# Token statistics taken from x^T, and attention operands transposed ahead on VectorE, in a hybrid convolution, attention and retention block

## The chip, the cores and the metric

The kernel runs on one core of a Trainium2 chip. Its time is that of one execution on the device, in microseconds (us); the smaller, the better. The engines are TensorE (PE, matrix products, with PEld for its weight loads), VectorE (DVE), ScalarE (ACT), GpSimd (POOL), and SyncE (SP), which here only issues DMAs. Each engine works off its own list of instructions in order.

## The reference

One layer of a trunk with 1024 tokens and 16 meta tokens put ahead of them, width 1024. All three groups of mixers read the same normalized input through one projection, and their outputs go through one output projection:

```
h = concat([meta, x])                         # 1040 x 1024
u = rms_norm(h, ln_w)                         # h * rsqrt(mean(h*h) + eps) * ln_w
cx, cb, cc, cz, cq, ckv, krope, mz, rq, rk, rv, rz = split(u @ w_in)
y_conv = cb * (conv_b + sum_j w[j] * (cc*cx)[t-2+j]) * silu(cz)
q = rms_norm(rms_norm(cq) @ w_uq)             # 8 heads of 96 (64 + 32 with rope)
k = rms_norm([rms_norm(ckv) @ w_ukv, krope])
o_mla = softmax(q k^T / sqrt(96), chunk causal) v * silu(mz)
o_ret = retention(rq, rk, rv) * silu(rz)      # 4 heads of 64, chunks of 64
h + concat([y_conv, o_mla, o_ret]) @ w_out    # without the meta tokens
```

All data are float32.

## The kernel before

Every large product is made in three: both factors are split into a high part, rounded to the PE's fp32r format, and a low part, the remainder (`split`: the high part on ACT, L103 or L106, the low part on DVE or POOL, L104, and L107 where a scale is applied), and `mm3` (L112) adds high x high, high x low and low x high. Products of 512 columns are the bulk of PE's work.

The stages follow one another in this order on PE:

- *Gate products* (`mz`, 0 to 55 us). x^T comes in eight tiles `xs` of 128 x 1040 (one per block k of 128 input features), which are split into `xah`, `xal`, `xbh`, `xbl`; the gate weights `ws_mz` come per k and are split into `wh_mz`, `wl_mz` (the low part on POOL for k = 2 and 5, else on DVE). The accumulators are eight tiles of 128 x 512, (b, g) for b = 0 to 3 and g = 0, 1; five of them are summed while the tiles arrive, the other three afterwards by `rest`.
- *Token statistics*. The mean square of a token is needed for each token as a row (`rb`, for tiles with tokens on the columns) and as a column (`r`). The kernel loads x once more with tokens on the partitions (`xt`, 16 loads of 256 KB on SP, L227), squares it on ACT with a running sum, and forms `vx`, `r` and, by a product with ones, the row `rps` (L243).
- *Latent projection* (`A`, 55 to about 135 us): weights `ws_A`, products `A`, and per block of tokens `a_lat` and `a_up`, which norm, apply rope and store q, k and v of all heads to DRAM (`q_s`, `k_s`, `v_s`), tokens on the rows.
- *Retention* (two units of 9 blocks, to about 245 us), *convolution* (two units, `conv_cx`, `conv_cz`, `conv_cb`, to about 343 us).
- *Attention* (to 531 us). The heads run one after the other; scores run four blocks ahead of the rest of a head. A head's operands `kT`, `qT` (features on the partitions, high and low, two buffers of each for alternate heads) are made by `qk_t` (L662): q and k of a pair of heads are loaded (`load_pair`), four 128 x 96 blocks are transposed on PE into PSUM (L668), and split from there on ACT and DVE. Heads 0 and 1 are prepared among the last convolution products, head h + 2 in four steps within head h.
- *Output projection* (to the end).

The gate results are finished one after the other behind the statistics (`mzz`, L257 to L260) and stored to DRAM (`mz_s`) on SP. The code gives the engines' work in program order, and a scheduler of the framework orders each engine's list ahead of time from this and from the dependencies; a `tc.issue_after` keeps an instruction behind another in that order.

Of the kernel before, what the change touches and what calls it, by code (L numbers as in the profile page):

```python
# [35 lines left out]
V_LN, V_QA, V_KVA, V_QN, V_KN, V_CW, V_CB, V_RN = 0, 8, 10, 11, 12, 13, 19, 21  # L36
NV = 22
# [13 lines left out]
def trunk(tc, ins, outs):  # L51
# [15 lines left out]
    NA, NW, GA = 4, 8, 0  # L67
# [13 lines left out]

    vec = cp.tile([P, NV], F32, name="vec")
# [12 lines left out]
    wqk = cp.tile([P, 1], F32, name="wqk")  # L95
# [13 lines left out]
    def mm3(out, l_, r_, first, last):  # L109

        for i, (x_, y_) in enumerate(((l_[0], r_[0]), (l_[0], r_[1]), (l_[1], r_[0]))):
            nc.tensor.matmul(out, lhsT=x_, rhs=y_, start=first and i == 0, stop=last and i == 2)  # L112
# [57 lines left out]
    with tc.tile_pool(name="ps0", bufs=1, space=PSUM, reuse_waits="tile") as ps0:  # L170
# [3 lines left out]
        warm2 = ps0.tile([P, 512], F32, tag="rps", name="warm2", bufs=2)  # L174
# [4 lines left out]
        def rest(b, g, a):  # L179
            for k in range(KT):  # L180
# [37 lines left out]
        ssh = cp.tile([P, 2, 9], F32, name="ssh")  # L218
        nc.gpsimd.memset(ssh, float(D // 2))
        for g, ts_ in enumerate(((0, 1, 2, 3), (4, 5, 6, 7), (8,))):  # L220
            for t in ts_:
                rows = NM if t == 8 else P
                src = meta_d if t == 8 else x_d[t * P:t * P + P]
                for j in range(2):
                    xt = work(("t3", "t4")[j], f"xt{t}_{j}")
# [3 lines left out]
            if g == GA:  # L229
                with tc.issue_after(last_t.ins):  # L230
                    wA = [load_w("A", k) for k in range(NA)]
            gs = slice(ts_[0], ts_[-1] + 1)
            nc.vector.tensor_tensor(vx[:, gs], ssh[:, 0, gs], ssh[:, 1, gs], op=ALU.add)
            nc.vector.tensor_scalar(vx[:, gs], vx[:, gs], 1.0 / D, EPS, op0=ALU.mult, op1=ALU.add)
            rsqrt(r[:, gs], vx[:, gs], len(ts_))
            if g == 2:
                break

            dg = work("t2", f"dg{g}").rearrange("p (t q) -> p t q", t=4)
            rps = ps0.tile([P, 512], F32, tag="rps", name=f"rps{g}", bufs=2)  # L240
# [8 lines left out]
        rest(2, 1, accs[2, 1])  # L249
        for g in range(2):  # L250
            accs[3, g] = ps0.tile([P, 512], F32, tag="rps", name=f"mz3{g}", bufs=2)
            rest(3, g, accs[3, g])
        for b in range(4):
            for g in range(2):
                z = work(("t3", "t4")[g], f"mzz{b}{g}")
# [4 lines left out]
                nc.sync.dma_start(mz_s[b][:, g * 512:g * 512 + 512], z)  # L260
# [8 lines left out]
    with tc.issue_after(last_t.ins):  # L269
        wA += [load_w("A", k) for k in range(len(wA), KT)]  # L270
# [4 lines left out]
    for i, (src, u_, j, sc) in enumerate([(wuq_d[:, 0, :], uq, 0, V_QA), (wuq_d[:, 1, :], uq, 1, V_QA + 1),  # L275
# [3 lines left out]
        with tc.issue_after(last_t.ins):  # L279
# [7 lines left out]
    nc.gpsimd.tensor_tensor(wqk, vec[:, V_QN:V_QN + 1], vec[:, V_KN:V_KN + 1], op=ALU.mult)  # L287
# [12 lines left out]

    def a_lat(t, ps):
# [5 lines left out]
        nc.vector.tensor_copy(c[R, c0:416], ps[R, c0:416])  # L307
# [95 lines left out]
    for t in [8] + list(range(NT)):  # L403
# [4 lines left out]
        if t == 3:  # L408
            wr = [[load_w("r0", k) for k in range(KT)]]
# [11 lines left out]
    oz = {}  # L421
# [9 lines left out]
    def r_rope(u, t, ps):  # L431
# [6 lines left out]
        nc.scalar.activation(rtf[R, cs], ps[R, cs], AF.Copy, scale=r[R, t:t + 1])  # L438
# [8 lines left out]
        nc.vector.tensor_tensor(qk[R, hs], qk[R, hs], tmp[R, hs], op=ALU.add)  # L447
# [87 lines left out]
    def feat(u, b, lo_, n, name):  # L535
# [3 lines left out]
        step()  # L539
        return pp  # L540

    def load_pair(hp):
        qt = hp_pool.tile([P, NT, 192], F32, tag="q", name=f"q{hp}")
        kt = hp_pool.tile([P, NT, 192], F32, tag="k", name=f"k{hp}")
        vt = hp_pool.tile([P, NT, 128], F32, tag="v", name=f"v{hp}")
        nc.sync.dma_start(kt, k_s.rearrange("t p c -> p t c")[:, :, hp * 192:hp * 192 + 192])
        nc.sync.dma_start(qt, q_s.rearrange("t p c -> p t c")[:, :, hp * 192:hp * 192 + 192])
        nc.sync.dma_start(vt, v_s[:SEQ, hp * 128:hp * 128 + 128].rearrange("(b p) c -> p b c", p=P))
        return qt, kt, vt
# [3 lines left out]
    def conv_cx(u, g, b):  # L553
# [3 lines left out]
        for lo_, n in (((NM - 2, 258), (NM + 256, 256)) if g == 0 else ((HA, 512),)):  # L557
# [11 lines left out]
    def conv_cz(u, g):  # L569
# [424 lines left out]
```

## Time and profile before

| | us |
|---|---|
| time, median of 3 runs | 579.41 |
| lowest and highest | 579.18, 580.03 |
| the profiled execution, its own time | 581.55 |
| its span in the profile | 579.8 |
| PE busy | 569.8 |
| DVE, ACT, POOL busy | 330.9, 255.0, 224.1 |

The rows come from one profiled execution, whose span begins with its first instruction; its own time is 1.75 us longer than the span. A row names a line of the kernel, the engine, the operation, and the tiles written and read, without the numbers of buffers.

### The profile page before, as it was taken

What the parts mean: (1) busy time and instruction counts of PE and PEld (TensorE: products, weight loads), DVE (VectorE), ACT (ScalarE), POOL (GpSimd) and SP (SyncE); (2) the same over time, 40 slices, a digit from 0 to 9 for tenths busy, and PEclk for the clock granted to TensorE, in tenths of its full rate; (3) what the DMA queues carried; (4) which work ended last, traced back from release to release, by engine and by line L of the source; (5) the groups of instructions that cost most, each with busy time, mean ns of one, the idle gap of its engine ahead of it and who ended that gap; (6) DMA issues with size and microseconds to landing.
All of it is one profiled execution on the core that took longest, in us unless ns stands there. A gap on an engine that the chain in (4) does not pass through costs nothing.

```text
span 579.8 us, 9595 instructions
## 1 busy us (share of the span) xinstructions
PE 569.8 (98%) x3401; PEld 481.7 (83%) x3401; DVE 330.9 (57%) x761; ACT 255.0 (44%) x616; POOL 224.1 (39%) x330
## 2 busy tenths in 40 slices
PE   8999999999999999999999999999999999999997
PEld 5877899988888888898898888898888888876886
DVE  5547768888536432553332667675757857664132
ACT  6765535665234332532010438475655646543000
POOL 2023258677103220151242968443524334624000
PEclk9999999999999999999999999999999999999999
DMA  8887513274703200130030648235112223113096
GB/s 326 289 265 241 182 67 120 108 224 158 234 1 92 74 0 19 54 110 18 20 97 1 199 145 273 73 103 171 56 38 73 77 71 128 37 68 116 1 301 224
DMA packets 46657, 70.39 MB, mean 121 GB/s; under 512 B 3792, under 2 KB 21840, under 8 KB 46480
## 3 DMA queue, kind: packets, MB, share of 16 engines
q1 hardware_dynamic: 43008, 63.47, 33.8%
q10 hardware_dynamic: 3600, 6.29, 2.9%
q8 instruction: 27, 0.44, 0.3%
q14 instruction: 22, 0.18, 0.1%
HBM read 48.75 MB, written 21.00 MB: 120 GB/s over the span
## 4 chain that ended last, share of the span: by engine, by line
PE 83%; DMA 9%; DVE 3%; ACT 2%; issue 2%; POOL 0%; SPq 0%; DVEq 0%; ACTq 0%; POOLq 0%
PE r L112 16%; PE S L112 9%; PE cv L112 8%; PE part L112 7%; PE A L112 6%; PE o L765 6%; PE pTp L724 5%; PE cz L112 4%; PE cb L112 4%; DMA out<-ot 4%; PE out L112 3%; PE qps L112 3%; DMA xs<-in_xT 2%; DMA xt<-in_x 2%; PE rsp L477 1%
## 5 line engine op out<-in xcount | busy, mean ns | idle before, releaser
L702 ACT ACTIVATE pr<-S,smx 128x144 f32<-128x144 f32 (+8 forms) x72 | 50.4, 701 | 27.3 <-DVE smx L693 13.4
L693 DVE TENSOR_REDUCE smx<-S 128x1 f32<-128x144 f32 (+8 forms) x72 | 49.8, 701 | 15.7 <-PE S L112 6.3
L710 POOL TENSOR_SCALAR pm<-pr,smx 128x16 f32<-128x16 f32 x64 | 18.4, 288 | 85.2 <-DVE smx L708 61.3
L711 POOL TENSOR_SCALAR pr<-pr,smx 128x128 f32<-128x128 f32 (+3 forms) x64 | 48.1, 752 | 0.6 <-DVE smx L708 0.6
L724 PE MATMUL pTp<-ident,pr 128*128 128x128 f32 x288 | 45.4, 274 | 1.5 <-ACT pt L730 1.4
L730 ACT COPY pt<-pTp 128x512 f32<-128x512 f32 (+2 forms) x64 | 31.8, 505 | 26.3 <-PE pTp L724 24.9
L451 POOL TENSOR_SCALAR kw<-qk,con 128x64 f32<-128x64 f32 (+1 forms) x36 | 13.8, 397 | 71.7 <-DVE qk L447 58.4
L724 PEld LDWEIGHTS pTp<-ident,pr 128*128 128x128 f32 x288 | 35.0, 140 | 7.0 <-POOL wol L104 1.8
L765 PEld LDWEIGHTS o<-pt,v 128*64 128x64 f32 x448 | 26.5, 137 | 12.1 <-issue 4.7
L765 PE MATMUL o<-pt,v 128*64 128x256 f32 (+2 forms) x448 | 36.2, 309 | 0.0
L112 PE MATMUL r<-wh_r,xal 128*128 128x512 f32 (+1 forms) x80 | 30.5, 381 | 0.0
L112 PE MATMUL r<-wh_r,xah 128*128 128x512 f32 (+1 forms) x80 | 30.4, 380 | 0.0
L112 PE MATMUL part<-woh,yh 128*128 128x512 f32 x64 | 30.1, 470 | 0.0
L112 PE MATMUL r<-wl_r,xah 128*128 128x512 f32 (+1 forms) x80 | 30.0, 375 | 0.0
L882 DVE SCALAR_TENSOR_TENSOR ot<-out,xr 128x512 f32<-128x512 f32 (+1 forms) x17 | 11.2, 660 | 31.1 <-DMA out<-ot 16.8
L112 PE MATMUL r<-wl_r,xbh 128*128 128x512 f32 x64 | 26.1, 409 | 0.0
L112 PE MATMUL r<-wh_r,xbh 128*128 128x512 f32 x64 | 25.7, 401 | 0.0
L112 PE MATMUL part<-wol,yh 128*128 128x512 f32 x64 | 25.5, 399 | 0.0
L112 PE MATMUL r<-wh_r,xbl 128*128 128x512 f32 x64 | 25.5, 398 | 0.0
L112 PE MATMUL part<-woh,yl 128*128 128x512 f32 x64 | 25.2, 394 | 0.0
L773 DVE TENSOR_TENSOR ym<-o,ym 64x256 f32<-64x256 f32 x32 | 13.5, 421 | 16.7 <-PE o L767 16.2
L104 POOL TENSOR_TENSOR wol<-wos,woh 128x512 fp32r<-128x512 f32 x16 | 20.4, 1291 | 2.6 <-ACT woh L103 2.6
(295 smaller groups left out, 1716.1 us busy)
## 6 DMA issues: line engine op xcount, KB each, us to landing
xt<-in_x SPq DMA_DIRECT2D x16, 256.0 KB, 4.5
ws_r<-in_win SPq DMA_DIRECT2D x16, 256.0 KB, 3.3
ws_c<-in_win SPq DMA_DIRECT2D x16, 256.0 KB, 2.9
wos<-in_wout SPq DMA_DIRECT2D x16, 256.0 KB, 3.8
xp<-in_x SPq DMA_DIRECT2D x16, 256.0 KB, 2.7
p_s<-xp SPq DMA_DIRECT2D x16, 256.0 KB, 2.0
xr<-p_s SPq DMA_DIRECT2D x15, 256.0 KB, 4.5
out<-ot ACTq DMA_DIRECT2D x15, 256.0 KB, 4.5
```

The lines of the kernel that those rows point to most:

```text
L104: (lo_eng or nc.vector).tensor_tensor(lo, src, hi.bitcast(F32), op=ALU.subtract)
L112: nc.tensor.matmul(out, lhsT=x_, rhs=y_, start=first and i == 0, stop=last and i == 2)
L451: nc.gpsimd.tensor_scalar(kw[R, j], qk[R, 2 + j], con[R, kd0 + j:kd0 + j + 1], 1.0, op0=ALU.mult, op1=ALU.mult)
L693: nc.vector.tensor_reduce(sm[:, i // 2:i // 2 + 1], sp[:, :n, :w], axis=AX.XY, op=ALU.max, negate=True)
L702: e = nc.scalar.activation(pr[:, c0:c1].rearrange("p (b c) -> p b c", b=n), sp, AF.Exp, bias=mx, accum_out=sm[:, 5 + i:6 + i])
L710: nc.gpsimd.tensor_scalar(pm[(2 * h + t // 4) % 2][:, t % 4, :NM], pr[:, nk - NM:nk], sm[:, 9:10], 1.0, op0=ALU.mult, op1=ALU.mult)
L711: nc.gpsimd.tensor_scalar(pr[:, :nk - NM], pr[:, :nk - NM], sm[:, 9:10], 1.0, op0=ALU.mult, op1=ALU.mult)
L724: tr_ = nc.tensor.transpose(out=tp[:, b * P:b * P + P], in_=pr[:, c0:c0 + P], identity=ident)
L730: nc.scalar.copy(pt[:, b0:b0 + nb, tt], src)
L765: nc.tensor.matmul(op[64 * cg:64 * cg + 64, c0:c1], lhsT=lv, rhs=src[:, i_, c_], start=b == 0, stop=False)
L773: nc.vector.tensor_tensor(ys, op[64 * cg:64 * cg + 64, :256].rearrange("p (a c q) -> p a c q", a=2, q=64), ys, op=ALU.mult)
L882: nc.vector.scalar_tensor_tensor(ot, acc[:, c0:c1], 0.5, xt, op0=ALU.mult, op1=ALU.add)
```

## The change

- *Statistics.* The loads `xt` and their squares go. ACT squares each x^T tile (`xsq`; the first one straight into the tile that later holds the constants, `con`), POOL adds the seven others to it, and nine products of 128 (or 16) tokens by a column of ones (`ssp`) sum over the features. The constants are loaded into `con` afterwards.
- *Weights and gate stores.* The loads of the A weights follow the last x^T tile; the gate results are kept and stored last. The remaining gate products run over k outside. Warm-up products: 11 instead of 8.
- *Queries and keys.* `qk_t` goes. `turn` handles k or q of a pair of heads in four parts, in slots spread over retention, convolution and the first steps of attention (`BEGIN`): it loads 128 x 8 x 192 from `k_s` or `q_s`, transposes it in blocks of 32 x 32 on DVE, splits it, and stores high and low part to DRAM (`T_s`). `load_head` fetches a head's `kT` and `qT` from there in 12 DMAs of 32 x 4 x 256 (128 KB).
- *Smaller ones.* The copy of `A` out of PSUM moves from DVE to ACT, one product in the convolution stands earlier on POOL, and the scale of some output weights is applied within the split.

The core of the diff:

```diff
-        accs = {bg: ps0.tile([P, 512], F32, name=f"mz{bg[0]}{bg[1]}") for bg in ((2, 1), (2, 0), (1, 1), (1, 0), (0, 1), (0, 0))}
+        ssp = bank("m31", "ssp")
...
+            if k == 0:
+                nc.scalar.activation(con[:, :L], st, AF.Square)
+            else:
+                sq = hp_pool.tile([P, L], F32, tag="v", name=f"xsq{k}")
+                nc.scalar.activation(sq, st, AF.Square)
+                nc.gpsimd.tensor_tensor(con[:, :L], con[:, :L], sq, op=ALU.add)
...
-                    with tc.issue_after(last_x.ins):
-                        last_t = nc.sync.dma_start(xt[:rows], src[:, j * 512:j * 512 + 512])
-                    nc.scalar.activation(xt[:rows], xt[:rows], AF.Square, accum_out=ssh[:rows, j, t:t + 1])
...
+        for t in range(9):
+            t0, rows = tok(t)
+            nc.tensor.matmul(ssp[:rows, t:t + 1], lhsT=con[:, t0:t0 + rows], rhs=ones[:, :1], start=True, stop=True)
...
-                nc.sync.dma_start(mz_s[b][:, g * 512:g * 512 + 512], z)
+                store.append((mz_s[b][:, g * 512:g * 512 + 512], z))
+        for x in store:
+            nc.sync.dma_start(*x)
...
-        nc.vector.tensor_copy(c[R, c0:416], ps[R, c0:416])
+        act[0] = nc.scalar.copy(c[R, c0:416], ps[R, c0:416]).ins
...
+    def turn(i, part):
+        hp, which = i // 2, 1 - i % 2
+        if part == 0:
+            src = hp_pool.tile([P, NT, 192], F32, tag="q", name=f"ts{i}")
...
+            for j, y in enumerate(x.rearrange("(j n r) c -> j r n c", j=4, r=32)):
+                nc.sync.dma_start(src[32 * j:32 * j + 32], y)
...
+                nc.vector.transpose(dst[:, 3 * j:3 * j + 3].rearrange("p c (n k) -> p n c k", k=32),
+                                    turned[i][0][:, :, 96 * j:96 * j + 96].rearrange("p n (c k) -> p n c k", k=32))
...
+    def load_head(h):
+        for which in (1, 0):
+            for x, src in zip((qT, kT)[which][h % 2], T_s[which][h // 2]):
...
+                for c in range(3):
+                    nc.sync.dma_start(x[32 * c:32 * c + 32, o:o + SEQ].bitcast(F32).rearrange("p (i r) -> p i r", i=4), src[3 * (h % 2) + c])
...
-            for j in range(4):
-                nc.tensor.transpose(out=tp[:96, j * P:j * P + P], in_=src[:, 4 * g + j, cs], identity=ident)
```

Three places in the engines' lists. The first is POOL at the start, from the product of two norm vectors (`wqk`) on: before, two low parts of gate weights stand there, and then the powers of the token statistics (`r`).

```order
L287 TENSOR_TENSOR wqk<-vec 128x1
L104 TENSOR_TENSOR wl_mz_209<-ws_mz_206,wh_mz_208 128x512
L104 TENSOR_TENSOR wl_mz_302<-ws_mz_299,wh_mz_301 128x512
L98 TENSOR_TENSOR r<-vx,half_neg 128x4
```

The changed kernel has the seven additions (`con` and `xsq`) around the same two.

```order
L309 TENSOR_TENSOR wqk<-vec 128x2
L225 TENSOR_TENSOR con<-con,xsq_182 128x1040
L106 TENSOR_TENSOR wl_mz_222<-ws_mz_219,wh_mz_221 128x512
L225 TENSOR_TENSOR con<-con,xsq_216 128x1040
L225 TENSOR_TENSOR con<-con,xsq_250 128x1040
L225 TENSOR_TENSOR con<-con,xsq_284 128x1040
L106 TENSOR_TENSOR wl_mz_324<-ws_mz_321,wh_mz_323 128x512
L225 TENSOR_TENSOR con<-con,xsq_318 128x1040
L225 TENSOR_TENSOR con<-con,xsq_352 128x1040
```

So POOL's second low part now stands behind four additions, and the one power `r` behind all seven. The second place is SP between the gate products and the latent projection; `ws_A` and `ws_r` are weights, `mz_s` the stored gates, `ust` weights of the heads' projections. Before:

```order
L280 DMA ust_647<-in_wuq 128x768
L260 DMA mz_s<-mzz_576 128x512
L260 DMA mz_s<-mzz_582 128x512
L118 DMA ws_A_631<-in_win 128x416
L118 DMA ws_r_1110<-in_win 128x512
L260 DMA mz_s<-mzz_588 128x512
L118 DMA ws_r_1116<-in_win 128x512
L280 DMA ust_651<-in_wukv 128x512
```

And in the changed kernel:

```order
L121 DMA ws_A_568<-in_win 128x416
L302 DMA ust_627<-in_wukv 128x512
L302 DMA ust_631<-in_wukv 128x512
L293 DMA con<-in_con 128x2254
L121 DMA ws_A_582<-in_win 128x416
L121 DMA ws_r_1086<-in_win 128x512
L121 DMA ws_r_1092<-in_win 128x512
L121 DMA ws_r_1098<-in_win 128x512
L283 DMA mz_s<-mzz_538 128x512 x3
```

The last `ws_A` stood behind five stores of gates; now it stands ahead of all of them, and behind the load of the constants (`con`). The third place is the end of the convolution, on PE, where `cb` and `cz` are convolution products and `S` are scores. Before, the transposes of a half of head 0 stand ahead of its fourth block of scores:

```order
L112 MATMUL cb_1_3508<-xbh_357,wl_c_2961 128x512
L668 MATMUL kTp_0_3535<-ident,k_3278 96x128 x4
L668 MATMUL qTp_0_3544<-ident,q_3277 96x128 x4
L112 MATMUL S_3_0_3619<-kt0h,qt0h 128x264
L112 MATMUL S_3_0_3619<-kt0l,qt0h 128x264
L112 MATMUL S_3_0_3619<-kt0h,qt0l 128x264
```

In the changed kernel the scores stand among the convolution products, with no transposes ahead of them:

```order
L114 MATMUL cz_1_3554<-xbh_246,wl_c_2994 128x512
L114 MATMUL cz_1_3554<-xbh_280,wh_c_2999 128x512
L114 MATMUL S_0_0_3537<-kt0h,qt0h 128x144
L114 MATMUL S_0_0_3537<-kt0l,qt0h 128x144
L114 MATMUL cz_1_3554<-xbl_281,wh_c_2999 128x512
L114 MATMUL cz_1_3554<-xbh_280,wl_c_3000 128x512
L114 MATMUL cz_1_3554<-xbh_314,wh_c_3005 128x512
L114 MATMUL S_0_0_3537<-kt0h,qt0l 128x144
```

The operands of these scores now come over SP, where before the loads of output weights (`wos`) and mixer results (`ysrc`) follow each other:

```order
L593 DMA y_s<-yv_0_3214 128x512
L609 DMA wos_0_3326<-in_wout 128x512
L609 DMA wos_0_3330<-in_wout 128x512
L609 DMA wos_0_3334<-in_wout 128x512
L609 DMA wos_0_3338<-in_wout 128x512
L779 DMA ysrc_3502<-y_s 128x4x128
L779 DMA ysrc_3658<-y_s 128x4x128
L790 DMA xp_0_3719<-in_x 128x512
```

In the changed kernel the 24 loads of heads 0 and 1 stand between them, each row three DMAs:

```order
L672 DMA y_s<-yv_0_3321 128x512
L688 DMA wos_0_3432<-in_wout 128x512
L688 DMA wos_0_3436<-in_wout 128x512
L688 DMA wos_0_3440<-in_wout 128x512
L688 DMA wos_0_3444<-in_wout 128x512
L621 DMA kt0h<-kT_s 32x4x256 x3
L621 DMA kt0l<-kT_s 32x4x256 x3
L621 DMA qt0h<-qT_s 32x4x256 x3
L621 DMA qt0l<-qT_s 32x4x256 x3
L621 DMA kt1h<-kT_s 32x4x256 x3
L621 DMA kt1l<-kT_s 32x4x256 x3
L621 DMA qt1h<-qT_s 32x4x256 x3
L621 DMA qt1l<-qT_s 32x4x256 x3
L582 DMA kT_s<-th_1_3502 128x768
```

The loads of `ysrc` have moved behind these and behind two stores of a turn.

## Rows read from the trace of the kernel before

**Rows 1.** The page: engines' busy time, and the chain that ended last.
```profile
PE 569.8 (98%) x3401; PEld 481.7 (83%) x3401; DVE 330.9 (57%) x761; ACT 255.0 (44%) x616; POOL 224.1 (39%) x330
...
PE 83%; DMA 9%; DVE 3%; ACT 2%; issue 2%; POOL 0%; SPq 0%; DVEq 0%; ACTq 0%; POOLq 0%
```

**Rows 2.** Windows: start:end, length, busy us (x instructions) by engine, PEclk, DMA share, GB/s.
```profile
0.00:20.00 20.00, 17.64 (x60) 12.34 (x61) 13.34 (x19) 13.79 (x22) 5.20 (x18) 1.00 0.90 322
20.00:40.00 20.00, 20.00 (x86) 15.91 (x85) 7.11 (x13) 15.48 (x43) 2.55 (x2) 1.00 0.78 263
...
245.00:320.00 75.00, 75.00 (x440) 65.98 (x439) 29.79 (x53) 14.42 (x31) 25.24 (x25) 1.00 0.16 48
...
400.00:520.00 120.00, 119.99 (x957) 101.34 (x953) 80.26 (x197) 68.06 (x165) 50.59 (x93) 1.00 0.21 71
```

**Rows 3.** What PE waits for: us in total, times, longest.
```profile
PE A L112 <- ACT wh_A L103: 1.5, 1, 1.5
...
PE A L112 <- DVE wl_A L104: 0.4, 1, 0.4
PE rps L243 <- DVE vxe L248: 0.3, 1, 0.3
```

**Rows 4.** Timeline of PE, end of the convolution: start, us, engine, line, operation, tile, count.
```profile
330.38 0.60 PE L668 MATMUL kTp<-ident,k 128*96 128x128 f32 x4
330.82 0.60 PE L668 MATMUL qTp<-ident,q 128*96 128x128 f32 x4
331.17 0.31 PE L112 MATMUL S<-kt0h,qt0h 104*128 104x144 f32 x1
```

**Rows 5.** Timeline of SP before the latent projection.
```profile
51.68 1.82 SPq L260 DMA_DIRECT2D mz_s<-mzz  x2
53.60 0.37 SPq L118 DMA_DIRECT2D ws_A<-in_win  x1
```

**Rows 6.** Timeline of PE in the retention.
```profile
204.06 0.55 PE L494 MATMUL rop<-rt,qs 128*128 128x64 f32 x4
204.44 0.39 PE L456 MATMUL rtp<-ident,qk 128*128 128x128 f32 x2
```

**Rows 7.** Timeline of DVE in the gate stage.
```profile
10.64 1.39 DVE L107 SCALAR_TENSOR_TENSOR xal<-xs,vec,xah 128x528 fp32r<-128x528 f32 x1 [0.33 <-ACT xah L106]
...
12.65 0.77 DVE L107 SCALAR_TENSOR_TENSOR xal<-xs,vec,xah 128x528 fp32r<-128x528 f32 x1
```

**Rows 8.** Timeline of POOL in the gate stage.
```profile
10.04 1.42 POOL L104 TENSOR_TENSOR wl_mz<-ws_mz,wh_mz 128x512 fp32r<-128x512 f32 x1 [4.87 <-ACT wh_mz L103]
```

**Rows 9.** Groups of POOL by form: operation, shapes, count | busy, mean ns | idle before.
```profile
L563 POOL TENSOR_TENSOR ccs<-ccs,rb 128x512 f32<-128x512 f32 x2 | 2.2, 1098 | 0.0
...
L563 POOL TENSOR_TENSOR ccs<-ccs,rb 128x256 f32<-128x256 f32 x2 | 1.3, 638 | 2.2 <-DVE ccs L562 2.2
```

**Rows 10.** Timeline of PE, the first gate products.
```profile
5.96 1.65 PE L112 MATMUL mz<-xah,wh_mz 128*128 128x512 f32 x3 [1.18 <-ACT wh_mz L103]
...
10.97 0.39 PE L112 MATMUL mz<-xbl,wh_mz 128*128 128x512 f32 x1
11.20 0.40 PE L112 MATMUL mz<-xbh,wl_mz 128*128 128x512 f32 x1
```

**Rows 11.** Groups of DVE by form.
```profile
L387 DVE TENSOR_TENSOR kqo<-kqo,scq 128x768 f32<-128x768 f32 x8 | 8.8, 1100 | 5.7 <-POOL scq L98 5.7
```

**Rows 12.** Chain that ended last in order of time: start, us, what.
```profile
398.45 3.03 PE o L765 x34
422.00 3.03 PE o L765 x34
```

**Rows 13.** Timeline of SP, end of the convolution.
```profile
320.06 1.80 SPq L609 DMA_DIRECT2D wos<-in_wout  x4
```

**Rows 14.** DMA issues: tile, queue, operation, count, KB each, median us to landing.
```profile
vr<-v_s SPq DMA_DIRECT2D x8, 32.0 KB, 6.5
xr<-p_s SPq DMA_DIRECT2D x2, 128.0 KB, 3.7
```

More of the change, by code (lines that the diff above doesn't have):

```diff
@@ L80, in trunk @@
     p_s = dp.tile([2, SEQ, 512], F32, name="p_s")
+    T_s = [dp.tile([4, 2, P, 6, 256], F32, name=f"{c}T_s") for c in "qk"]
     vec = cp.tile([P, NV], F32, name="vec")
@@ L111, in mm3 @@
         for i, (x_, y_) in enumerate(((l_[0], r_[0]), (l_[0], r_[1]), (l_[1], r_[0]))):
-            nc.tensor.matmul(out, lhsT=x_, rhs=y_, start=first and i == 0, stop=last and i == 2)
+            m = nc.tensor.matmul(out, lhsT=x_, rhs=y_, start=first and i == 0, stop=last and i == 2)
+        return m.ins
     def load_w(u, k, eng=None, between=None):
@@ L173, in trunk @@
         nc.vector.memset(warm, 0.0)
-        warm2 = ps0.tile([P, 512], F32, tag="rps", name="warm2", bufs=2)
+        bank = lambda tag, name: ps0.tile([P, 512], F32, tag=tag, name=name)
+        accs = {(b, g): bank(f"m{b}{g}", f"mz{b}{g}") for b in (1, 2) for g in range(2)}
+        warm2 = bank("m30", "warm2")
         for i in range(NW):
@@ L266, in pst @@
         return (psj if tag == "pj" else psw).tile([P, 512], F32, tag=tag, name=name)
-    with tc.issue_after(last_t.ins):
-        wA += [load_w("A", k) for k in range(len(wA), KT)]
+    with tc.issue_after(last_x.ins):
         nc.sync.dma_start(con, ins["con"])
@@ L408, in trunk @@
         if t == 3:
-            wr = [[load_w("r0", k) for k in range(KT)]]
+            with tc.issue_after(act[0]):
+                wr = [[load_w("r0", k) for k in range(KT)]]
     rA = con[:, C_RA:C_RB].rearrange("p (t d) -> p t d", t=9)
@@ L522, in r_norm, with turns @@
         later(fin)
+    turned, slot = {}, [0]
+    BEGIN = (3, 6, 10, 17, 21, 25, 29, 36)
+    def turn(i, part):
+        hp, which = i // 2, 1 - i % 2
+        if part == 0:
+            src = hp_pool.tile([P, NT, 192], F32, tag="q", name=f"ts{i}")
+            x = (q_s, k_s)[which].rearrange("t p c -> (t p) c")[:, hp * 192:hp * 192 + 192]
+            for j, y in enumerate(x.rearrange("(j n r) c -> j r n c", j=4, r=32)):
+                nc.sync.dma_start(src[32 * j:32 * j + 32], y)
+            turned[i] = [src]
+        elif part == 1:
+            dst = hp_pool.tile([P, 6, 256], F32, tag="q", name=f"td{i}")
+            for j in range(2):
+                nc.vector.transpose(dst[:, 3 * j:3 * j + 3].rearrange("p c (n k) -> p n c k", k=32),
+                                    turned[i][0][:, :, 96 * j:96 * j + 96].rearrange("p n (c k) -> p n c k", k=32))
+            turned[i] = [dst]
+        elif part == 2:
+            dst = turned[i][0]
+            for j in range(2):
+                hi = hp_pool.tile([P, 3, 256], F32R, tag="v" if i < 6 else "k", name=f"th{i}_{j}")
+                x = dst[:, 3 * j:3 * j + 3]
+                if which:
+                    split(hi, x.bitcast(F32R), x)
+                else:
+                    for c in range(3):
+                        split(hi[:, c], x[:, c].bitcast(F32R), x[:, c], scale=wqk[:, c:c + 1] if c < 2 else None)
+                turned[i].append(hi)
+        else:
+            dst, *hi = turned.pop(i)
+            for j in range(2):
+                nc.sync.dma_start(T_s[which][hp, 0, :, 3 * j:3 * j + 3], hi[j].bitcast(F32))
+            nc.sync.dma_start(T_s[which][hp, 1], dst)
+    def turns():
+        n = slot[0]
+        slot[0] += 1
+        for ago, part in ((4, 3), (3, 2), (2, 1), (0, 0)):
+            if n - ago in BEGIN:
+                with tc.issue_after(at["act" if part == 2 else "dve"]):
+                    turn(BEGIN.index(n - ago), part)
     for u in range(2):
@@ L527, in trunk @@
             step()
+            if t != 8:
+                turns()
             if t == 3:
@@ L797, in trunk @@
     cuts = [load_wo(k, 0) for k in (0, 1, 6, 7)]
+    for h in range(2):
+        load_head(h)
     conv_cx(1, 1, 1)
-    qk_t(0, 0, 1)
-    qk_t(0, 0, 0)
     conv_cx(1, 1, 0)
-    qk_t(0, 1, 1)
-    qk_t(0, 1, 0)
     score(0, 0)
@@ L811, in trunk @@
     conv_cb(1, 1)
-    for g in range(2):
-        qk_t(1, g, 1)
-        qk_t(1, g, 0)
     step()
@@ L840, in trunk @@
             p_t(h, t)
+            turns()
             if t == 0 and h in (0, 2, 4):
                 pairs.append(load_pair(h // 2 + 1))
-            for i, a in enumerate(QK):
-                if h + 2 < H and t == a:
-                    qk_t(h + 2, *((0, 1), (0, 0), (1, 1), (1, 0))[i])
+            if t == QK and h + 2 < H:
+                load_head(h + 2)
         if 1 <= n and seq[n - 1][1] % 4 == 3:
@@ L964, in _layout @@
     qn, kn = A["q_norm"][0], A["k_norm"][0]
[L965 to L966 removed]
+    for o, n in ((V_QN, qn), (V_KN, kn)):
+        vec[:, o:o + 2] = np.tile(n[:64].reshape(2, 32).T, (4, 1))
     for u in range(2):
```

123 lines of the change are left out of this document (57 added, 66 removed).

## The prediction

> **What bounds the kernel now.** I read the page first: TensorE (PE) is busy for 98% of the span and makes up 83% of the chain that ended last [rows 1]. Next the windows, to see whether that average hides stages with another limit: PE stands at 119.99 of 120 us in the heads between 400 and 520, and only the first 20 us have a gap that matters [rows 2]. The table of what PE waits for is short: 1.5 and 0.4 us before the latent projection (tile A), 0.3 us for the row of token scales [rows 3]. So the time is the sum of what PE has to issue, plus those waits. Work taken from PE comes back in full as long as VectorE (DVE), ScalarE (ACT), GpSimd (POOL) and the DMAs still deliver on time, and these have room in the mean: 80, 68 and 51 of 120 us in the heads [rows 2].
>
> **What the change removes.** *Transposes.* 128 PE transposes go, 32 groups of four. A group's price is read from the starts: 330.38, 330.82 and 331.17 for kTp, qTp and what follows, so 0.44 and 0.35 [rows 4]. Taking 0.40, 32 groups give 12.8 us; with 0.36 or 0.45 throughout, 11.5 or 14.4. Eight groups lie in the convolution and 24 (9.6 us) in the heads. The 32 splits out of PSUM on ACT and as many on DVE go with them.
>
> *Waits ahead of A.* The eighth A weight is issued on SP at 53.60, behind two gate stores [rows 5]; PE's waits of 1.5 and 0.4 [rows 3] are for its split. With the gate stores last and A's loads ahead of them, both go: −1.9. The last A load is now queued behind that of the constants, which waits for the new sums (about 45 by the walk below), and is wanted when the gate products end (about 59), so it stays hidden with some 10 us. The 0.3 us wait for the row of scales goes too, since the other gate products lie between the statistics and that row. If the loads were late for another reason, these 2.2 us stay.
>
> **What it adds on PE.** Nine f32 products with a one-column right side (ssp). A float32 product of this kernel is two PE instructions, and four short ones (128x64) at 204.06 take 0.38 us until the next instruction [rows 6], so 0.095 each; 18 of them 1.7 us. Bounds: 0.9 if each product is one instruction, 3.4 if none overlaps its neighbour and each costs twice as much. I take 1.6. The three extra warm-up products lie before the first real one.
>
> **What it adds on the other engines in the first 40 us.** ACT squares eight x^T tiles of 128x1040; POOL sums them with seven adds of 128x1040, while DVE makes the low parts of x and of the gate weights, which PE waits for. DVE is busy 13.3 us and POOL 5.2 us in the first 20 now [rows 2], so shares alone would leave room. But two rows speak against that: the split of x costs 0.77 us at 12.65 and 1.39 at 10.64 [rows 7], and ahead of this one POOL runs its own subtraction from 10.04 to 11.46 [rows 8] (a second such pair, at 18 us, reads the same). The slow split ends at 12.03, 0.57 us after POOL's end: it stood still until POOL was through, then ran at its usual pitch (0.68 from start to start). So two-operand work from SBUF on these two engines alternates here. Price of an add: POOL's in-place product takes 1.10 us for 128x512 and 0.64 for 128x256 [rows 9], by which 1040 elements are 2.05; the subtraction's 1.42 scales to 2.88 at most. I take 2.4, between; seven are 17 us.
>
> Walked by hand: x tiles come as now; ACT works off its operations one after the other (22 in 13.79 us, 0.63 each [rows 2], a square of double width 1.15). The first sum can start at about 10.9. From there POOL (2.4 per add, 1.3 for a weight) and DVE (0.68 per split) take turns. The three splits for k=3 end at 19.1, 22.1 and 25.1, those of k=4 at 27.1, 30.2 and 30.9. PE starts at 5.96, issues its first twelve products 0.418 us apart (5.96 to 10.97) and later ones 0.23 apart [rows 10]; with 59 products for k=0 to 2 it wants k=3 at 21.8 and waits 2.4 us for its last split, and wants k=4 at 27.7 and waits 2.3. From k=5 on POOL has run dry now and then (the squares have two buffers and ACT is in order), DVE leads, and PE waits no more: the last add ends at 41.4, PE comes to ssp at 43.7. Sum +4.7; with adds of 2.1 it is 3.2, with 2.7 it is 6.2, and nothing if the adds do not hold DVE up.
>
> [...]
>
> *The clock.* That the first twelve products run at half pace costs 2.3 us (12 x 0.19). Eleven warm-up products instead of eight can close the gap of 1.18 us ahead of the first product [rows 10], and then the 2.3 come back. In the walk they are lost again: PE only arrives at k=3 sooner, and k=3's splits set the time. Counted at 0 here.
>
> **What it adds later.** Eight turns between 150 and 345: per turn two DVE transposes of 768 elements per partition, splits and three stores. The trace of before has no such DVE operation; the nearest row is 1.10 us for 768 elements [rows 11]; I bound it by half and by four times that. Sixteen of them are 17.6 us of DVE (9 to 70), spread over some 190 us, of which the convolution shows it busy for 29.8 of 75 [rows 2]; hidden at any of these prices, the splits standing against the 32 that it is spared. Nothing of PE waits for a turn until a head's first score.
>
> The loads of a head are 12 DMAs of 128 KB on SP. For heads 2 to 7 they are issued at the sixth step of the head two before; a head takes 23.55 us now (422.00 less 398.45 [rows 12]), so about 20 us later they are wanted: 12 issues of 0.45 (four in 1.80 [rows 13]) are 5.4, landing another 3.7 to 6.5 (128 KB in full rows, and 32 KB into 16 partitions [rows 14]), so 8 us are to spare. The head that is tight is head 0: its loads come behind the four wos loads, which are issued up to 321.9 [rows 13], so they go out until 327.3 and land by 331.0 to 333.8, and its first score, 64 products of 0.23 us after 318.6, stands at 333.3. Between nothing and 0.5 us; with what head 1, the rows behind it and new waits in retention can cost, I take +0.5, up to 3.
>
> [...]
>
> **Sum.** −12.8 −1.9 −0.3 +1.6 +4.7 +0.5 = −8.2. The profiled execution took 581.55 us for a span of 579.8, so it lies 2.1 above the median of 579.41; the sum is applied to the median: 571.2, say 571.
>
> **Rivals.**
> *A, the adds are hidden* (chance 0.25). POOL's adds hold DVE up less, or late splits find PE late too. For it: DVE and POOL together are busy for 28 of the first 40 us now [rows 2]. Against it: the slow split [rows 7, 8]. Without the 4.7: 566.5; with the warm clock from the first product another 2.3: 564.
> *B, the heads give part back* (0.18). With PE's 1.6 us per head gone, the loop from score through maximum, exponent and transposition to the output sets the pace, or scores wait for loads. For it: DVE is at 80 of 120, and its work comes in bursts per head. Against it: PE has practically no wait there [rows 2], and DVE and ACT are relieved of the splits of these same groups. Half of the 9.6 us gone: 576.
> *C, slower* (0.07). ACT runs in order, and each square waits for a buffer that an add must free; the next split of x stands behind that square. If DVE loses every turn and POOL's backlog passes on through ACT, PE waits for each of the seven adds in full: at 2.7 us that is 18.9 in place of 4.7, and 585.4. It decides from 12.9 us of waiting, 1.85 per add. Against it: PE has 44 us of gate products in that stretch, and the adds total 17.
> *D, no net change* (0.03): mixtures of B and C at 579.
>
> **How the numbers follow.** The sum has a chance of 0.47, with a range of its own from 568 to 574 (adds 2.1 to 2.7, transposes at their bounds). To leave out no more than 2 in 10, the range takes in A with the clock (564 less 1) and B with adds of 2.7 (577.5). A measurement of this kernel can tell about 0.2% (1.2 us) from no change: faster has the sum, A and nearly all of B, 0.89; same 0.04; slower 0.07.
>
> **What would show it.** Right: no transposes of q and k, heads spaced about 21.9 us; splits of x at 3 us in DVE's rows with POOL adds under them, of about 2.4 us each; PE waits at k=3 and k=4 for DVE, 4 to 5 us together; no wait ahead of A; ssp under 2 us. Wrong: adds of 2 us without slow splits (A), new waits of PE for S, pt or the head loads (B), PE waiting at every k (C).

## The result, and the profile after

The changed kernel takes 585.98 us (584.81 to 586.59, 4 runs) against 579.72 us of the kernel before, measured beside it: ratio 1.0105, 95% interval 1.0084 to 1.0127. It is 6.3 us slower where 8.4 us less were forecast. The profiled execution has a span of 583.6 us, 3.8 more than before; the profiled execution of before lies 2.1 us above its median, that of the changed kernel 0.5 below its own, so traces show less of the loss than the times.

On the page of the changed kernel PE is busy for 3.4 us less than before [rows 1], where the forecast took 12.8 away and put 1.6 on, and for a smaller share of the span:

```profile
PE 566.4 (97%) x3294; PEld 473.7 (81%) x3294; DVE 353.6 (61%) x769; ACT 255.0 (44%) x598; POOL 235.4 (40%) x327
```

The windows (columns as in [rows 2]) show where it is late. PE loses 6.3 us between 20 and 40, with a granted clock of 0.91 and 0.92 there and in the next window; it now has gaps between 340 and 400, where it had none (20.00 and 40.00 us busy in these two windows); and in the heads, 400 to 520, it is as full as before, with fewer instructions:

```profile
0.00:20.00 20.00, 18.81 (x72) 13.04 (x73) 13.19 (x11) 15.49 (x23) 12.20 (x20) 1.00 0.72 266
20.00:40.00 20.00, 13.69 (x52) 10.27 (x51) 19.40 (x15) 9.54 (x14) 12.64 (x5) 0.91 0.34 110
40.00:60.00 20.00, 20.00 (x87) 15.77 (x87) 10.02 (x19) 7.21 (x12) 6.46 (x7) 0.92 0.54 170
...
245.00:320.00 75.00, 74.07 (x439) 65.14 (x438) 45.28 (x83) 25.62 (x58) 24.76 (x23) 1.00 0.54 176
...
340.00:360.00 20.00, 17.57 (x87) 14.37 (x86) 7.55 (x17) 6.30 (x17) 10.27 (x17) 1.00 0.96 268
360.00:400.00 40.00, 37.78 (x274) 30.01 (x274) 29.59 (x73) 23.67 (x61) 19.62 (x35) 1.00 0.76 228
400.00:520.00 120.00, 120.00 (x905) 100.17 (x902) 74.46 (x187) 64.32 (x158) 54.42 (x103) 1.00 0.45 128
```

What PE waits for (as [rows 3]): the waits ahead of A are gone, and new ones stand at the gate products and at the start of the attention:

```profile
PE mz L114 <- DVE wl_mz L106: 6.0, 1, 6.0
PE S L114 <- ACT pr L762: 1.9, 1, 1.9
PE pTp L784 <- POOL pr L771: 1.7, 1, 1.7
...
PE cv L114 <- DVE ccs L641: 0.9, 1, 0.9
PE S L114 <- DMA qt0l<-qT_s: 0.6, 2, 0.4
```

*The gate products.* DVE's splits next to POOL's additions, first DVE, then POOL:

```profile
30.42 2.89 DVE L109 SCALAR_TENSOR_TENSOR xbl<-xs,vec,xbh 128x512 fp32r<-128x512 f32 x1
33.23 2.87 DVE L109 SCALAR_TENSOR_TENSOR xal<-xs,vec,xah 128x528 fp32r<-128x528 f32 x1
...
36.69 1.28 DVE L106 TENSOR_TENSOR wl_mz<-ws_mz,wh_mz 128x512 fp32r<-128x512 f32 x2
```

```profile
22.75 2.62 POOL L225 TENSOR_TENSOR con<-con,xsq 128x1040 f32<-128x1040 f32 x1 [2.78 <-ACT xsq L224]
...
27.05 8.49 POOL L225 TENSOR_TENSOR con<-con,xsq 128x1040 f32<-128x1040 f32 x3
```

A split takes 2.9 us where an addition is under way when it comes up (0.77 otherwise [rows 7]), and three additions in a row (2.8 each) let one split through after each. The low parts of the last weights (36.69) come last on DVE, and PE, which had run ahead, needs the one of k = 6 at 31.2:

```profile
5.74 0.96 PE L114 MATMUL mz<-xah,wh_mz 128*128 128x512 f32 x3
...
31.00 0.39 PE L114 MATMUL mz<-xal,wh_mz 128*128 128x512 f32 x1
37.42 0.79 PE L114 MATMUL mz<-xah,wl_mz 128*128 128x512 f32 x1 [6.03 <-DVE wl_mz L106]
38.01 0.63 PE L114 MATMUL mz<-xbh,wh_mz 128*128 128x512 f32 x1
...
42.71 0.57 PE L114 MATMUL mz<-xah,wl_mz 128*128 128x512 f32 x1
43.11 0.39 PE L114 MATMUL mz<-xah,wh_mz 128*128 128x512 f32 x1
```

The first product starts at 5.74 with no half-pace stretch behind it: the next group follows after 0.80 for three, where it took 1.45 [rows 10]. Then PE stands still for 6.03 us, and the thirteen products behind the wait are 0.43 us apart, before they return to 0.23: 2.7 us more. The granted clock of that stretch is 0.50:

```profile
37.50:42.70 5.20, 5.20 (x12) 4.04 (x13) 3.20 (x5) 1.61 (x3) 1.07 (x1) 0.50 0.74 218
```

The sums cost 1.90 us, from 46.58 to 48.48:

```profile
46.58 1.97 PE L242 MATMUL ssp<-ones,con 128*128 128x1 f32 x18
48.48 0.50 PE L114 MATMUL mz<-xbh,wl_mz 128*128 128x512 f32 x1
```

*The start of the attention.* The loads of heads 0 and 1 occupy SP from 331.66; the mixer results, ysrc, are issued behind them at 347.08 (at 321.97 before), and in these 15 us the DMAs are busy all the time (a share of 1.06 by the view, at 241 GB/s; from 330 to 340, 1.05 at 263):

```profile
331.66 1.30 SPq L621 DMA_DIRECT2D kt0h<-kT_s  x3
...
347.08 0.63 SPq L839 DMA_DIRECT2D ysrc<-y_s  x1
```

```profile
330.00:340.00 10.00, 10.00 (x45) 8.01 (x44) 7.17 (x9) 3.50 (x5) 4.96 (x9) 1.00 1.05 263
```

ACT converts ysrc at 352.84, after standing still for 6.32 us, and the exponent of a score row stands behind that conversion in its list:

```profile
352.84 0.62 ACT L105 CAST yh<-ysrc 128x512 fp32r<-128x512 f32 x1 [6.32 <-DMA ysrc<-y_s]
353.37 0.59 ACT L762 ACTIVATE pr<-S,smx 128x400 f32<-128x400 f32 x1
```

PE's next score needs the buffer which that exponent reads, and waits 1.85 us:

```profile
354.10 0.42 PE L114 MATMUL S<-kt0h,qt0h 104*128 104x328 f32 x1 [1.85 <-ACT pr L762]
```

*The heads.* PE's list has changed in a way that no term of the forecast spoke of. The o products of a half head (attention weights times v) come in pieces, with single transposes of softmax rows between them; 34 pieces in all, where before there were 19:

```profile
479.46 0.60 PE L784 MATMUL pTp<-ident,pr 128*128 128x128 f32 x4
479.99 1.37 PE L825 MATMUL o<-pt,v 128*64 128x256 f32 x20
481.29 0.33 PE L784 MATMUL pTp<-ident,pr 128*128 128x128 f32 x1
481.55 0.44 PE L827 MATMUL o<-ptm,vr 128*64 128x128 f32 x4
481.92 0.66 PE L784 MATMUL pTp<-ident,pr 128*128 128x128 f32 x4
```

Such a block comes 22.48 us after the one of the head before (in the chain that ended last):

```profile
457.58 1.30 PE o L825 x18
...
480.06 1.30 PE o L825 x18
```

That is 1.07 less than before [rows 12], where the four groups of transposes would give 1.6.

### The profile page after: what moved, and what is told of

Read it like the earlier page. It is cut to its first block, busy times and chain, and to the rows that moved or that the text cites. A ratio compares the mean times of both kernels' runs of the same rounds, so it can differ in the third digit from the quotient of the medians.

```text
span 583.6 us, 9535 instructions
## 1 busy us (share of the span) xinstructions
PE 566.4 (97%) x3294; PEld 473.7 (81%) x3294; DVE 353.6 (61%) x769; ACT 255.0 (44%) x598; POOL 235.4 (40%) x327
## 4 chain that ended last, share of the span: by engine, by line
PE 84%; DVE 3%; DMA 2%; POOL 1%; ACT 1%; issue 1%; SPq 0%; DVEq 0%; ACTq 0%; POOLq 0%
PE r L114 16%; PE S L114 8%; PE out L114 8%; PE part L114 7%; PE A L114 7%; PE o L825 6%; PE cv L114 6%; PE pTp L784 5%; PE mz L114 4%; PE cz L114 3%; PE qps L114 3%; PE cb L114 3%; PE kps L114 1%; PE vps L114 1%; PE rsp L502 1%; PE rop L519 1%
## 5 line engine op out<-in xcount | busy, mean ns | idle before, releaser
L476 POOL TENSOR_SCALAR kw<-qk,con 128x64 f32<-128x64 f32 (+1 forms) x36 | 16.3, 466 | 66.4 <-DVE qk L472 57.8
L825 PE MATMUL o<-pt,v 128*64 128x256 f32 (+2 forms) x448 | 38.9, 311 | 0.0
L114 PE MATMUL r<-wh_r,xal 128*128 128x512 f32 (+1 forms) x80 | 29.8, 373 | 0.0
L938 DVE SCALAR_TENSOR_TENSOR ot<-out,xr 128x512 f32<-128x512 f32 (+1 forms) x17 | 11.2, 660 | 30.5 <-PE out L114 17.4
L225 POOL TENSOR_TENSOR con<-con,xsq 128x1040 f32<-128x1040 f32 x7 | 19.1, 2724 | 8.1 <-ACT xsq L224 7.9
```

The source lines that it names most:

```text
L114: m = nc.tensor.matmul(out, lhsT=x_, rhs=y_, start=first and i == 0, stop=last and i == 2)
L225: nc.gpsimd.tensor_tensor(con[:, :L], con[:, :L], sq, op=ALU.add)
L476: nc.gpsimd.tensor_scalar(kw[R, j], qk[R, 2 + j], con[R, kd0 + j:kd0 + j + 1], 1.0, op0=ALU.mult, op1=ALU.mult)
L825: nc.tensor.matmul(op[64 * cg:64 * cg + 64, c0:c1], lhsT=lv, rhs=src[:, i_, c_], start=b == 0, stop=False)
L938: nc.vector.scalar_tensor_tensor(ot, acc[:, c0:c1], 0.5, xt, op0=ALU.mult, op1=ALU.add)
```

## Experiments

Each run has its ratio to the kernel before, measured beside it, with its 95% interval; the medians of before were 580.4 to 581.2 there.

**The statistics alone.** The kernel before, with the code of `ps0` (gate products, statistics, loads and stores around them) from the changed kernel and nothing else of it.

> The kernel before with the statistics part alone (squares of x^T tiles, sums on POOL, ssp, weights and gate stores reordered, 11 warm-up products), queries and keys as before. Theory, the whole loss to the start of the latent projection (6.6 us) comes from this part: 585 to 587. Rival, the trace's shift at that place is given back later since other engines catch up: 580 to 582.

Measured 587.21 us, ratio 1.0125 (1.0090 to 1.0161). The wait is there, as long as in the changed kernel:

```profile
PE mz L112 <- DVE wl_mz L104: 6.0, 1, 6.0
```

So this part costs all that the change costs, and queries and keys give nothing on balance.

**Without the additions.**

```diff
-                nc.gpsimd.tensor_tensor(con[:, :L], con[:, :L], sq, op=ALU.add)
```

> The changed kernel without the seven additions on POOL (the sum then holds the first tile's squares alone; ACT still squares all tiles). Theory, the additions hold the splits on DVE up: PE's wait of 6.0 us at 31.4 and the half-pace products behind it (2.7 us) go, DVE's splits cost 0.7 us again, and the time is 577 to 578. Rival, it is the squares, which stand ahead of later splits on the in-order ACT: PE still waits 3 us or more before 40, and the time is 582 or more.

576.71 us, 0.9947 (0.9924 to 0.9970), PE full from 20 to 60 us. The squares on ACT do not hold PE up; the additions do.

**The additions on DVE.**

```diff
-                nc.gpsimd.tensor_tensor(con[:, :L], con[:, :L], sq, op=ALU.add)
+                nc.vector.tensor_tensor(con[:, :L], con[:, :L], sq, op=ALU.add)
```

> The changed kernel with the seven additions on DVE instead of POOL. Theory, alternation of the two engines is what costs: DVE gets 7 x 1.3 = 9 us more to do but every split takes 0.7 again, DVE is busy for some 24 of 38 us, PE waits less than 2 us before 45, and the time is 578 to 580. Rival, any place for the additions ahead of the splits costs as much: 584 or more.

578.06 us, 0.9964 (0.9943 to 0.9984), as the theory had it. On DVE an addition takes 1.23 us and the split behind it its usual time:

```profile
23.39 1.23 DVE L225 TENSOR_TENSOR con<-con,xsq 128x1040 f32<-128x1040 f32 x1
24.54 0.75 DVE L109 SCALAR_TENSOR_TENSOR xal<-xs,vec,xah 128x528 fp32r<-128x528 f32 x1
```

PE waits for nothing between 6 and 60 us. The same work costs some 8 us less on the busier engine, because the two no longer take turns. The next runs start from this kernel unless they say otherwise.

**Queries and keys alone.** The changed kernel with the `ps0` code of before.

> The changed kernel with the statistics part of before: only queries and keys are moved to DVE and the head loads (and the small edits behind the latent projection). Theory, what the trace shows from there on (0.3 lost in the retention, 1.3 in the convolution, 3.3 and 0.5 gained behind it): 576.5 to 578.5. Rival, the sum of the forecast (12.8 less, 0.5 lost) is lost only because the late start shifts the work against the DMAs: 567 to 570.

581.94 us, 1.0021 (0.9997 to 1.0045): worse than both. The late start is not the cause. From the end of the third `cb` block in the convolution to the first output product this run takes 210.7 us where the kernel before takes 212.8, though 12.5 us of transposes are gone from that stretch, and 1.8 us are lost between the latent projection and there.

**The price of the transposes.**

```diff
-            for j in range(4):
+            for j in range(8):
-                nc.tensor.transpose(out=tp[:96, j * P:j * P + P], in_=src[:, 4 * g + j, cs], identity=ident)
+                nc.tensor.transpose(out=tp[:96, j % 4 * P:j % 4 * P + P], in_=src[:, 4 * g + j % 4, cs], identity=ident)
```

> The kernel before with each of the 128 transposes of queries and keys made twice. Theory, a group of four is 0.40 us of PE's time: 12 to 13 us more, 592 to 593. Rival, part of the groups lies in time in which PE would wait for the softmax rows: 8 us more or less, 588 at most.

594.53 us, 1.0241 (1.0207 to 1.0275): 14 us more, slightly above what was expected. A group of eight takes 0.87 and 0.79 us, about twice a group of four [rows 4]:

```profile
332.94 1.03 PE L668 MATMUL kTp<-ident,k 128*96 128x128 f32 x8
333.81 1.04 PE L668 MATMUL qTp<-ident,q 128*96 128x128 f32 x8
334.60 0.31 PE L112 MATMUL S<-kt0h,qt0h 104*128 104x144 f32 x1
```

So the 12.8 us were real work of PE.

**The loads of the later heads.** `load_head(h + 2)` left out in the loop of the heads, so that heads 2 to 7 score with the operands of heads 0 and 1.

> The changed kernel with the additions on DVE, without the loads of heads 2 to 7 (72 DMAs, 9.4 MB; these heads score with the operands of heads 0 and 1). Theory, the loads are hidden: within 1 us of 578.1, heads 22.5 apart. Rival, they crowd SP's queue or the DMAs: 575 or less.

578.61 us, 0.9964 (0.9944 to 0.9983), the same as with them: hidden.

**The o products in one block.**

```diff
-            attend(seq[n - 1][0], seq[n - 1][1] // 4)
+            with tc.issue_after(late["pe"]):
+                attend(seq[n - 1][0], seq[n - 1][1] // 4)
```

> The changed kernel with the additions on DVE (578.1 before), and each o product block kept behind the transposes of the row ahead, so that PE's list passes between transposes and o 23 times instead of 49 (16 in the kernel before). Theory, each such passage costs about 0.17 us in place of nothing (four transposes ahead of o take 0.53 from start to start, ahead of a score 0.36): 3 to 4.5 us less, 574 to 575, and heads 22.0 us apart. Rival, the heads are paced by the chain from score to output: heads stay 22.5 apart and the time within 1 us of 578.

576.25 us, 0.9911 (0.9883 to 0.9940), the fastest full kernel here, and faster than the kernel before. By the ratio that is 3.1 us less than without the edit, by the medians 1.8. Heads are 21.8 us apart. The same edit in the changed kernel itself, additions on POOL:

> The changed kernel as it is (additions on POOL, 586.0), with the o products kept behind the transposes. Theory, the order costs the same here as with the additions on DVE: heads 21.8 apart and 2 to 4 us less, 582 to 584. Rival, it was part of that kernel's own timing: heads stay 22.5 apart or the time stays above 585.

584.29 us, 1.0058 (1.0033 to 1.0083). The ratio falls by 0.0047, 2.7 us; the median alone, measured at another time, by 1.7. (The profiled execution is the fastest of its ten, 581.83 us, with the highest granted clock of them, 0.994; the others go down to 0.985.) Transposes, o products and again transposes now stand in blocks, and o blocks are 21.81 us apart:

```profile
476.01 0.98 PE L784 MATMUL pTp<-ident,pr 128*128 128x128 f32 x5
476.92 1.37 PE L825 MATMUL o<-pt,v 128*64 128x256 f32 x20
478.07 0.44 PE L827 MATMUL o<-ptm,vr 128*64 128x128 f32 x4
478.44 0.88 PE L784 MATMUL pTp<-ident,pr 128*128 128x128 f32 x6
```

```profile
455.18 1.30 PE o L825 x18
...
476.99 1.30 PE o L825 x18
```

**The order of SP's loads.** First, ysrc ahead of the 24 head loads (`y_split(0)` moved ahead of `load_head`):

> The changed kernel with the additions on DVE, and the first load of mixer results (ysrc) issued ahead of the 24 loads of heads 0 and 1. Theory, the queue of these loads on SP makes the partial products late and leaves PE without work between the first exponents: 1.5 to 3 us less than 578.1, and the waits of 1.7 and 1.7 us between 345 and 375 shrink. Rival, those waits are the chain of the first softmax rows itself, with nothing to put between: 577.5 to 578.5, same waits.

578.51 us, 0.9964 (0.9932 to 0.9995). Missed: the wait for an exponent is still 1.7 us. In this run's trace ACT stands still 3.9 us for the second ysrc instead, issued at 341.92 behind the head loads and four of wos. Then, from that run, both loads of ysrc ahead of head 1's:

```diff
     y_split(0)
-    for h in range(2):
-        load_head(h)
+    load_head(0)
...
+            if n == 0:
+                load_head(1)
```

> The changed kernel with the additions on DVE (578.1), with the first two loads of mixer results ahead of the loads of head 1, which are issued behind the first row of head 0. In the changed kernel ACT stands still for 6.3 us at the conversion of ysrc, which comes over SP behind 24 head loads, with the exponents of head 0 behind it. Theory, this is where PE's wait of 1.7 to 1.9 us for an exponent (pr) comes from: it goes, 1.5 to 2.5 us less, 575.6 to 576.6. Rival, the first exponents are the pace whatever ACT converts: a wait of 1.5 us or more stays and the time is within 1 us of 578.1.

581.40 us, 1.0008 (0.9981 to 1.0034), slower by 2.6 us in the ratio, though the intervals overlap slightly. That wait shrinks to 0.8 and 0.4 us, and the next late transfer takes its place, the small loads vr, which the o products need:

```profile
360.96 0.60 PE L827 MATMUL o<-ptm,vr 128*64 128x128 f32 x4 [4.19 <-DMA vr<-v_s]
```

With the o products in one block:

> Additions on DVE, o products kept behind transposes, and head 1's loads later, all three. If the causes are separate their gains add: 578.1 less 2.4 (o products, as measured) less 2 = 573.5 to 574.5. If not, 576 as with the o products alone.

577.22 us, 0.9945 (0.9925 to 0.9966): no gain over the block alone (0.9911). And on queries and keys alone:

> Queries and keys part alone (statistics as before; 581.9), with the same two orders as the run before: o products kept behind transposes, head 1's loads later. Theory, these two are what ate the 12.8 us of the removed transposes: 4 to 6 us less, 576 to 578. Rival, the loss is in the retention and convolution (turns on DVE): 580 or more.

579.69 us, 0.9975 (0.9948 to 1.0003): between the two. Then other queues; first `vr` on ACT's (`nc.scalar.dma_start`), then head 1 there too:

> All three fixes (577.2), with the eight small loads vr issued by ACT's queue instead of SP's. Theory, with head 1's loads moved, vr was the next transfer to come late on SP (PE waited 3.2 us for it): that wait goes, 574 to 575.5. Rival, the DMAs themselves are full there and vr lands as late from any queue: wait of 2 us or more, 576.5 or more.

580.91 us, 0.9994 (0.9975 to 1.0012). The wait for vr goes, but PE waits 4.8 us for an exponent: the issues stand on ACT ahead of it.

> As the run before, and the 12 loads of head 1 issued by ACT's queue, together with those of head 0 on SP's. Theory, SP's queue as the cause: ysrc, wos and vr are all on time, waits between 330 and 390 under 2 us, 572.5 to 574.5. Rival, the DMAs' capacity as the cause: the loads of both heads crowd each other, the first score waits over 1 us for its operands, 576 or more.

580.43 us, 0.9980 (0.9960 to 1.0000): waits of 2.4 us for head 0's operands, as the rival had it, and 2.4 for an exponent behind the issues of vr. The DMAs are busy all the time between 320 and 340 here too (shares of 1.04 and 1.05), which speaks for their capacity. Since in both runs the issues on ACT make waits of their own, the queue's part is not told apart.

**Without the first loads.**

```diff
-    for h in range(2):
-        load_head(h)
+    for x in kT + qT:
+        for y in x:
+            nc.vector.memset(y[:96].bitcast(F32), 0.0)
```

> Additions on DVE and o products kept behind transposes (576.3), without the 24 loads of heads 0 and 1: their operands are filled with zeros on DVE instead, so heads 0 and 1 score zeros. Theory, PE's waits between 330 and 390 (4 to 5 us: for an exponent behind a late ysrc, for weights wos, for scores' operands) come from these 3.1 MB standing on SP ahead of everything else there: they go but for 1 us, and the time is 572 to 573.5. Rival, the first softmax rows set the pace there: 3 us of waits stay and the time is 575 or more.

579.27 us, 0.9963 (0.9942 to 0.9984), and inconclusive: the eight fills on DVE made PE wait 2.1 us for operands and 3.2 us for the buffer of a convolution product. With the fills on POOL:

> As the run without the loads of heads 0 and 1, the zeros now written on POOL, since on DVE the eight fills stood ahead of a convolution product's copy and made new waits of 2.1 and 3.2 us. Theory, the loads cause PE's waits between 330 and 390: at most 2 us of waits there, and 572 to 574 against the 576.3 with the loads. Rival, the first softmax rows set the pace: 3 us or more of waits, 575 or more.

572.86 us, 0.9854 (0.9821 to 0.9886), 3.3 us less than with the loads (0.9911). The wait for an exponent is 0.4 us, where it was 1.8; the longest that is left there is for a weight:

```profile
PE part L114 <- ACT woh L108: 1.7, 1, 1.7
...
PE S L114 <- ACT pr L762: 0.4, 1, 0.4
```

So the loads of heads 0 and 1 cause the wait for the exponent, and the first softmax rows do not set the pace. They do not cause all waits: of 4.9 us between 325 and 400 with the loads, 3.5 are left, 1.1 of them (for the buffer of a convolution product) new in this run. What the time gained beyond that is no wait; the granted clock from the third `cb` block to the first output product is 0.99 here and 0.98 in the trace with the loads.

**Warm-up products.** `NW` 8 in place of 11, on the kernel with both orders:

> All three as in the run before the last, with 8 warm-up products instead of 11. Theory, the three more close the gap ahead of the first gate product and spare its half-pace start: 2.0 to 2.5 us more than with 11. Rival, splits set the time there anyway: no difference above 0.7 us.

578.13 us, 0.9954 (0.9930 to 0.9977) against 0.9945 with 11: not told apart. In the traces the latent projection starts at 56.2 instead of 54.2, so 2.0 us at that place; in the time it stays open.

## Why the prediction was wrong

**What failed** is the step from PE's work to the time: "Work taken from PE comes back in full as long as [the others] still deliver on time", with 0.5 us set against it. I take the stretch from the last product of the third `cb` block to the first output product. It lasts 212.8 us before, 209.5 after, and 206.0 in the changed kernel with the o products in one block. Taking off PE's waits in it (1.4, 5.0 and 6.4 us), PE's own work is 211.4, 204.5 and 199.6. With the transposes' 12.5 us in it gone, 198.9 were due, and the run with the block comes within 0.7. The windows of this stretch, for the three traces in this order:

```profile
318.38:531.40 213.02, 211.56 (x1570) 178.35 (x1568) 141.72 (x325) 119.46 (x285) 110.63 (x186) 1.00 0.34 108
...
325.97:535.60 209.63, 204.36 (x1442) 167.31 (x1440) 129.94 (x306) 107.55 (x260) 101.91 (x178) 1.00 0.59 168
...
325.86:532.00 206.14, 199.00 (x1442) 166.19 (x1440) 128.48 (x306) 107.54 (x260) 102.24 (x178) 1.00 0.60 170
```

The last two have the same 1442 products at the full granted clock, and PE is busy for 5.4 us less in the last (the ends of products are modelled there; by starts and waits it is the 4.9 of 204.5 less 199.6). With the additions on DVE the same pair gives 205.8 and 202.9 us of PE's own work, at granted clocks of 0.99 and 0.98. So:

- 4.9 us are the order of PE's list, and 0.7 are not explained. The list passes between transposes and o products 16 times before, 49 times after and 24 times with the block; if these passages are the price, 25 fewer are worth 0.2 us each. That is not shown: the pieces of o products, with any neighbour, go 19, 34 and 17, and PE takes some 0.2 us from the last product of a piece to whatever follows, and 0.07 within a piece. In time the block gave back less than 4.9 (3.5 in these traces, 2.7 by the ratio), since the waits grew by 1.4. I read the two lists and compared which instructions stand in them, not in which company.
- 3.6 us are new waits (5.0 less the 1.4 of before, which are gone). For 2.4 of the 5.0 the cause is shown, the 24 loads on SP: 1.85 for the exponent behind ysrc, and 0.4 and 0.2 for head 0's operands, near the forecast's "Between nothing and 0.5 us". What is queued behind these loads (ysrc, wos, vr) the forecast had in the same 0.5 ("the rows behind it", up to 3), without asking what stands behind their conversion on ACT. The cause of the third wait, 1.7 for a softmax row from POOL, stays open: it does not go with any order of the loads, and is gone in the runs with the o products in one block, which have other waits.

Against the forecast's 200.8 for this stretch (212.8 − 12.5 + 0.5) the changed kernel is 8.7 us late (4.9 + 0.7 + 3.6 − 0.5). With 2.5 at the gate products (next paragraph) that is 11.2 of the 12.0 us between −8.2 and the span's +3.8. Of the other 0.8, 0.9 lie between the two places (259.5 us before, 260.4 after, with a wait of 0.9 for DVE in the convolution), −0.4 in the output (48.4 and 47.9), and 0.3 are transposes, 12.5 in place of 12.8.

**Right mechanism, wrong size:** the additions. That additions and splits take turns was right, and adds took 2.7 us instead of 2.4. But by hand PE waited at k = 3 and 4, in two pieces, and the last addition ended at 41.4; in the trace it ends at 35.5, and the list put the low parts for k = 6 and 7 behind all splits of x, so PE waited once, for 6.2 us with a small one instead of 4.7. Some 2.5 of these it waited because its products had started 0.2 us sooner and at full pace. Then it paid 2.7 us at half pace, for which the sum had nothing. Rows 7 and 8 showed the turn for a subtraction of 1.42 us; that a split stands behind a whole addition as well was the forecast's assumption, and the trace after shows it, with splits of 2.9 us beside additions of 2.7. Up to the first full product of the latent projection the forecast had +4.1 (−1.9 −0.3 +1.6 +4.7); it came at 65.55 instead of 58.91, +6.6, so 2.5 more. Of these, 2.0 are 1.5 of waiting, 2.7 at half pace and 0.3 in the sums, less the 2.5 of the faster start; 0.5 are not placed.

**Right:** the waits ahead of A are gone. The sums cost 1.9 (1.6 was taken). The 2.3 us of the half-pace start came back, and were lost again in the wait, since the splits set the time. The transposes on DVE are cheap:

```profile
L564 DVE STREAM_TRANSPOSE td<-ts 128x768 f32<-128x768 f32 x16 | 14.6, 953 | 0.0
```

They do not lie quite free in the convolution, though: DVE goes from 29.8 [rows 2] to 45.3 of 75 us there, and PE waits 0.9 us for it. That was not tried by itself.

**The rivals.** B came true in part, by its loads and by the order of PE's list, which it did not name; not by the chain from score to output. C's 585.4 is near the time by chance, since its mechanism did not happen: PE stood still once, for 6.2 us in all and not 18.9, and the larger part of what is missing lies in the attention. A's hidden additions came only with the additions on DVE, and its 566.5 not even then (578.06).

## What to carry to other kernels

Work that is put on an idle engine can stop a busy one, as POOL's additions of 2.7 us did here (splits of 2.9 us on DVE in place of 0.77): before counting it as hidden, look for a pair of rows in which the two overlap, and price the turns they take. When many transfers are put ahead of others on a queue, follow not only who needs the new ones but what stands behind the late ones on each in-order engine. And when work is taken from the engine that bounds, compare what stands next to what in its new list: here 4.9 of the 12.5 us taken from PE were lost again by order alone.

## What was not expected of the hardware

After a standstill of 6.03 us PE ran thirteen products at 0.43 us apart, half the pace of 0.23, at a granted clock of 0.50. A granted clock below 1 is also seen after shorter waits between 340 and 400 in some runs: 0.91 and 0.96 in the windows 340 to 360 and 360 to 400 of the run with the o products in one block and the additions on DVE, after waits of 1.8 and 1.5 us (products 0.43 us apart again, from 347.47 to 350.03). But it is not seen behind the changed kernel's waits of 1.85 and 1.7 us (1.00 in both windows), nor in the kernel before behind a wait of 1.5 us ahead of A (1.00 from 56 to 62). What decides between them is not shown; it makes a short wait cost more than itself in some runs. The loads into 32 partitions landed in 3.3 to 4.3 us for 128 KB in the median, where the forecast took 3.7 to 6.5. But while those of heads 0 and 1 were issued the DMAs were busy all the time (a share of 1.06) at 241 GB/s, where the first 20 us of the kernel before moved 322 GB/s at a share of 0.90 [rows 2]. Whether the 32 partitions are the reason was not tried.
